# A two-layer diffusion backbone on one core: another list scheduler for every engine but TensorE

## The chip, the cores and the metric

The kernel runs on one core of one Trainium2 chip. The metric is the device time of one execution in microseconds (us); lower is better. Each time is the median of several runs, and one more execution is recorded by the hardware profiler.

## The reference

Two layers work on 512 latent tokens `x` and 256 context tokens `ctx`, with a width of 1024. Each layer modulates its input by rows made from a conditioning vector, mixes tokens by attention, normalises, and then does the same around an MLP:

```python
for i in range(2):
    mod_x = silu(c) @ w_ada[i] + b_ada[i]            # 6 rows of 1024: shift, scale, gate, twice
    mod_c = silu(c_ctx) @ w_ada[i] + b_ada[i]
    hx, hc = x * (1 + sc1) + sh1, ctx * (1 + csc1) + csh1
    if i == 0: ax, ac = window_gqa(hx, hc, ...)      # 16 heads on 2 KV heads, band of 128, a sink logit
    else:      ax, ac = diff_attention(hx, hc, ...)  # 8 heads, softmax minus lambda times softmax
    x  = layer_norm(alpha * x + g1 * ax)
    fx = square(relu((x * (1 + sc2) + sh2) @ w1[i])) @ w2[i]
    x  = layer_norm(alpha * x + g2 * fx)
    # the context tokens take the same path in layer 0; layer 1 needs only x
```

## The kernel before

**Products.** Matmuls are float32 with both operands split into a rounded part and a rest. `wsplit` (line 302) loads a weight piece `w_raw` by DMA, makes the rounded part `w_h` by a copy on ScalarE (recorded at the helper's line 264), and the rest `w_l = w_raw - w_h` on VectorE (line 314). `mm3` (lines 325 to 327) issues the three matmuls of such a product. Loads use three buffers (`NRAW`), so a load is issued when an earlier piece has been split. In the first MLP the pieces are combined first: `w_half` and `w_sum` are such combinations, and `hx0m`, `hx_sum` and `hid` the activations' parts.

**Stages.** In the order of the profile: loads and modulation rows of layer 0 (to about 75 us), layer-0 attention (to 341), layer norm (to 381), first MLP (to 870) with the modulation rows of layer 1 done beside it, layer norm and the first projection of layer 1 (to 905), layer-1 attention (to 1285), layer norm (to 1330), second MLP (to the end).

**Layer norm.** The tokens are six tiles of 128 (`acc0_3734` to `acc0_3739` are the tiles of the layer-0 residual at the first norm, `acc0_7901` to `acc0_7906` at the second, `acc1_12804` to `acc1_12807` the four of layer 1). A sublayer's result in PSUM is multiplied by the gate (`g_tmp`, line 583, VectorE) and added to `acc`, on VectorE or POOL; BN_STATS, BN_AGGR and `rstd` give the moments (the power is on POOL); line 534 normalises the tile on VectorE; line 549 transposes it on TensorE (`xn_t`); ScalarE modulates the transposed tile (`fx`, `hx_v`) and rounds it (`hx0m`, `hx1`, `hx1m`), and VectorE makes the rest under the same name. `acc0 * g10 + g11` (line 672) makes the scaled residual afterwards.

**Modulation rows.** For layer 1 they are computed on VectorE beside the first MLP: each of 56 loads of `w_adaT` into `w_raw` is multiplied by the broadcast conditioning rows `cB0` and `cB1` and summed along the row (`ada_pr` or `w_raw`, an instruction printed as ISA in the order and as CUSTOM_DVE in the profile, then a read of its accumulator into `mods1` or `ada_half`).

**Attention of layer 1.** `sk` and `sq` are the rotated keys and queries, made on VectorE from `rope1`; line 1654 transposes `sk` on TensorE (`kT_ps`).

**What sets the order.** Each engine works through one row of instructions in program order. The row of TensorE is written out by the kernel's own planner (`Flow`), and is kept as written:

```python
ctx.enter_context(tc.manual_schedule(engines={mybir.EngineType.PE}))
```

The rows of VectorE (DVE), ScalarE (ACT), POOL and SyncE (SP, which issues the DMAs) are chosen by the framework's scheduler, which goes through all instructions with estimated times and picks, engine by engine, which of those that are ready goes next. A few hints (`add_manual_dep`) fix the order of single pairs.

## Time and profile before

| | us |
|---|---|
| median of 3 runs | 1657.44 (1653.25 to 1660.99) |
| profiled execution, its time | 1661.91 |
| its span in the profile | 1660.1 |
| TensorE (PE) busy | 1582.9 |
| VectorE (DVE) busy | 1134.4 |
| ScalarE (ACT) busy | 794.1 |
| POOL busy | 447.4 |
| moved by DMA | 181.17 MB |

The span is the time from the first to the last instruction of the profile; the rest of the execution's time lies around it. TensorE is busy for most of the span, so a time is lost where TensorE waits. In the lists of waits a row names the waiting engine with its line, what it waited for, the sum of the waits in us, how often, and the longest. In a timeline a row has its start, its length, engine, line, operation, and in brackets the idle time ahead of it with the instruction that ended it.

### The profile page before, as it was taken

What the parts mean: (1) busy time and instruction counts of PE and PEld (TensorE: products, weight loads), DVE (VectorE), ACT (ScalarE), POOL (GpSimd) and SP (SyncE); (2) the same over time, 40 slices, a digit from 0 to 9 for tenths busy, and PEclk for the clock granted to TensorE, in tenths of its full rate; (3) what the DMA queues carried; (4) which work ended last, traced back from release to release, by engine and by line L of the source; (5) the groups of instructions that cost most, each with busy time, mean ns of one, the idle gap of its engine ahead of it and who ended that gap; (6) DMA issues with size and microseconds to landing.
All of it is one profiled execution on the core that took longest, in us unless ns stands there. A gap on an engine that the chain in (4) does not pass through costs nothing.

```text
span 1660.1 us, 25174 instructions
## 1 busy us (share of the span) xinstructions
PE 1582.9 (95%) x9465; PEld 1384.8 (83%) x9465; DVE 1134.4 (68%) x2201; ACT 794.1 (48%) x1683; POOL 447.4 (27%) x369
## 2 busy tenths in 40 slices
PE   7899999989999999999997999999989799999998
PEld 5788777789788888889986999899877788888896
DVE  4655676689776688766566777677664886666667
ACT  3455675365343344334416555555552745555550
POOL 1333554106111121211191222220100033333363
PEclk9999999999999999999998999999899999999999
DMA  9110550533354434443323122211123233333221
GB/s 373 41 52 33 179 178 26 197 127 128 131 173 150 142 105 161 153 140 114 126 69 114 49 72 66 73 47 39 48 69 135 89 115 115 102 102 100 99 70 63
DMA packets 66434, 181.17 MB, mean 109 GB/s; under 512 B 7368, under 2 KB 13320, under 8 KB 66312
## 3 DMA queue, kind: packets, MB, share of 16 engines
q1 hardware_dynamic: 66312, 179.56, 32.0%
q8 instruction: 74, 1.21, 0.3%
q14 instruction: 48, 0.39, 0.1%
HBM read 168.49 MB, written 11.04 MB: 108 GB/s over the span
## 4 chain that ended last, share of the span: by engine, by line
PE 64%; DVE 14%; issue 7%; DMA 6%; POOL 5%; ACT 4%; SPq 0%; DVEq 0%; POOLq 0%; ACTq 0%
PE y_ps L327 8%; PE y_ps L325 8%; PE y_ps L326 7%; PE h_ps L325 6%; PE h_ps L326 6%; PE h_ps L327 6%; DMA w_raw<-in_w_adaT 3%; PE qkv_ps L325 2%; PE qkv_ps L326 2%; PE qkv_ps L327 2%; PE o_ps L1371 2%; PE s_ps L1750 2%; PE pT_ps L1389 2%; DVE w_l L314 2%; DVE w_raw L260 2%
## 5 line engine op out<-in xcount | busy, mean ns | idle before, releaser
L325 PE MATMUL y_ps<-w_h,hid 128*128 128x512 f32 (+1 forms) x648 | 257.4, 397 | 3.2 <-DVE fx L260 2.1
L327 PE MATMUL y_ps<-w_h,hid 128*128 128x512 f32 (+1 forms) x648 | 256.6, 396 | 2.7 <-DVE hid L260 2.6
L326 PE MATMUL y_ps<-w_l,hid 128*128 128x512 f32 (+1 forms) x648 | 255.8, 395 | 0.0
L314 DVE TENSOR_TENSOR w_l<-w_raw,w_h 128x1024 fp32r<-128x1024 f32 (+1 forms) x133 | 159.2, 1208 | 52.5 <-ACT w_h L264 49.9
L264 ACT CAST w_h<-w_raw 128x1024 fp32r<-128x1024 f32 (+1 forms) x133 | 131.2, 1001 | 94.8 <-PE y_ps L327 64.7
L264 ACT CAST w_half<-w_raw 128x512 fp32r<-128x512 f32 x130 | 80.3, 621 | 151.6 <-PE h_ps L327 106.2
L327 PEld LDWEIGHTS y_ps<-w_h,hid 128*128 128x128 f32 x648 | 122.8, 189 | 33.4 <-DVE hid L260 4.5
L325 PEld LDWEIGHTS y_ps<-w_h,hid 128*128 128x128 f32 x648 | 123.1, 190 | 29.1 <-DVE fx L260 2.5
L326 PEld LDWEIGHTS y_ps<-w_l,hid 128*128 128x128 f32 x648 | 123.1, 190 | 24.7
L260 DVE TENSOR_TENSOR w_half<-w_raw,w_half 128x512 fp32r<-128x512 f32 x130 | 106.6, 825 | 54.2 <-ACT w_half L264 53.8
L268 POOL TENSOR_TENSOR w_sum<-w_raw 128x512 f32<-128x512 f32 x26 | 58.2, 2238 | 316.9 <-DMA w_raw<-in_w 203.4
L325 PE MATMUL qkv_ps<-w_h,hx 128*128 128x384 f32 (+1 forms) x384 | 128.8, 335 | 2.8 <-ACT w_h L264 2.7
L326 PE MATMUL qkv_ps<-w_l,hx 128*128 128x384 f32 (+1 forms) x384 | 124.0, 323 | 2.0 <-DVE w_l L314 2.0
L327 PE MATMUL qkv_ps<-w_h,hx 128*128 128x384 f32 (+1 forms) x384 | 123.7, 322 | 0.0
L268 POOL TENSOR_TENSOR e<-e,sm 128x512 f32<-128x512 f32 (+2 forms) x96 | 92.6, 976 | 109.2 <-DVE sm L260 84.1
L260 DVE CUSTOM_DVE_ANT_0 w_raw<-w_raw,cB 128x512 f32<-128x512 f32 x112 | 83.1, 769 | 47.4 <-DMA w_raw<-in_w_adaT 47.2
L264 ACT ACTIVATE relu<-relu 128x384 f32<-128x384 f32 (+3 forms) x104 | 69.8, 673 | 64.5 <-DVE relu L260 62.9
L260 DVE TENSOR_TENSOR fx<-y_ps,fx 128x512 f32<-128x512 f32 x110 | 75.0, 686 | 36.9 <-PE y_ps L327 36.8
L268 POOL TENSOR_TENSOR rope<-rope,rope 128x256 f32<-128x256 f32 (+1 forms) x40 | 33.8, 846 | 224.7 <-DVE rope L260 178.0
L268 POOL TENSOR_TENSOR w_raw<-w_raw,w_sum 128x512 f32<-128x512 f32 x26 | 37.6, 1445 | 177.0 <-DVE w_half L260 154.7
L264 ACT ACTIVATE e<-e,nm 128x513 f32<-128x513 f32 (+2 forms) x96 | 65.9, 688 | 33.0 <-DVE nm L260 26.3
L325 PEld LDWEIGHTS qkv_ps<-w_h,hx 128*128 128x128 f32 x384 | 73.4, 191 | 4.6 <-ACT w_h L264 2.9
(268 smaller groups left out, 4323.5 us busy)
## 6 DMA issues: line engine op xcount, KB each, us to landing
w_raw<-in_w SPq DMA_DIRECT2D x128, 512.0 KB, 3.6
w_raw<-in_w_adaT SPq DMA_DIRECT2D x56, 512.0 KB, 3.8
w_raw<-in_w_ada SPq DMA_DIRECT2D x24, 512.0 KB, 4.3
w_raw<-in_b_w SPq DMA_DIRECT2D x32, 384.0 KB, 3.4
raw<-in_w_ada SPq DMA_DIRECT2D x16, 512.0 KB, 9.3
w_raw<-in_a_wq SPq DMA_DIRECT2D x8, 512.0 KB, 8.1
w_raw<-in_a_wo SPq DMA_DIRECT2D x8, 512.0 KB, 4.5
w_raw<-in_b_wo SPq DMA_DIRECT2D x8, 512.0 KB, 4.1
```

What stands on the lines that cost most here:

```text
L260: fn(**kw)
L264: fn(**kw)
L268: fn(**kw)
L314: last["split"] = nc.vector.tensor_tensor(**kw)
L325: nc.tensor.matmul(out=o, lhsT=lh, rhs=rh, start=start, stop=False, **kw)
L326: nc.tensor.matmul(out=o, lhsT=lh, rhs=rl, start=False, stop=False, **kw)
L327: last["pe"] = nc.tensor.matmul(out=o, lhsT=ll, rhs=rh, start=False, stop=stop, **kw)
L1371: nc.tensor.matmul(out=po[odd * HD:odd * HD + HD, 0:256], lhsT=vv[:, kb, kvh], rhs=pt_[:, odd * 256:odd * 256 + 256], start=(i == 0), stop ...
L1389: nc.tensor.transpose(out=pp[:, c * P:(c + 1) * P], in_=es[j][:, i * P:(i + 1) * P], identity=ident)
L1750: nc.tensor.matmul(out=sp[:, c * 512:c * 512 + 384], lhsT=qTt[:, tt, hl, qb * P:(qb + 1) * P], rhs=kS[:, tt, c * 384:c * 384 + 384], start ...
```

## The change

The scheduler is told to keep its time with its finer timeline model instead of its coarse one:

```diff
-    with tile.TileContext(nc) as tc:
+    with tile.TileContext(nc, schedule_with_timeline_sim=True) as tc:
```

The instructions stay the same, and so does TensorE's row. On the other engines the rows are permuted: nearly all of the difference is the place at which an instruction stands. Three places follow.

**VectorE at the norm before the first MLP.** `acc0_3739` is the last of the six tiles. Before, its statistics and its normalisation (last row) stood thus:

```order
L260 BN_STATS bn_3694<-acc0_3739 128x6
L260 TENSOR_TENSOR hx0m_3761<-fx_3765,hx0m_3761 128x2x128 x4
L260 BN_AGGR mv_4086<-bn_3694 128x2
L260 TENSOR_TENSOR fx_3762<-fx_3765,fx_3762 128x512
L260 TENSOR_SCALAR g11_3742<-g11_3742 128x1024
L260 TENSOR_SCALAR rstd_4088<-mv_4086 128x1
L260 TENSOR_TENSOR hx0m_3761<-fx_3766,hx0m_3761 128x2x128
L534 TENSOR_SCALAR acc0_3739<-acc0_3739,mv_4086,rstd_4088 128x1024
```

Now, from the row in which a weight split has come in:

```order
L314 TENSOR_TENSOR w_l_4410<-w_raw_4408,w_h_4409 128x1024
L260 TENSOR_TENSOR hx0m_3761<-fx_3765,hx0m_3761 128x2x128
L260 BN_AGGR mv_4086<-bn_3694 128x2
L260 TENSOR_TENSOR hx0m_3761<-fx_3765,hx0m_3761 128x2x128
L260 TENSOR_TENSOR fx_3765<-fx_3765 128x512
L260 TENSOR_SCALAR g11_3742<-g11_3742 128x1024
L260 TENSOR_TENSOR fx_3763<-fx_3766,fx_3763 128x512
L672 TENSOR_TENSOR acc0_3734<-acc0_3734,g10_3740 128x1024
L260 TENSOR_SCALAR rstd_4088<-mv_4086 128x1
L260 TENSOR_TENSOR fx_3765<-fx_3765,fx_3762 128x512
L260 TENSOR_TENSOR hx0m_3761<-fx_3766,hx0m_3761 128x2x128 x4
L260 TENSOR_TENSOR acc0_3734<-acc0_3734,g11_3742 128x1024
```

The normalisation of `acc0_3739` is the row behind the last one shown; ahead of it have come `w_l_4410`, the scaled residual of another tile (`acc0_3734`), steps of `fx`, and three more of `hx0m`.

**VectorE in the first MLP.** `relu_4778` and `relu_4777` are parts of the hidden activations, `w_raw_5164` is one of the 56 modulation loads. Before:

```order
L260 TENSOR_TENSOR relu_4778<-h_ps_4863,relu_4778 128x384
L260 TENSOR_TENSOR w_half_4939<-w_sum_4336,w_half_4939 128x512
L260 ISA w_raw_5142,mods1_82<-w_raw_5142,cB1_4675 128x512
L260 ISA mods1_82 128x1
L314 TENSOR_TENSOR w_l_4944<-w_raw_4942,w_h_4943 128x1024
L260 ISA ada_pr_5166,mods1_82<-w_raw_5164,cB0_4674 128x512
```

Now:

```order
L260 ISA ada_pr_5166,mods1_82<-w_raw_5164,cB0_4674 128x512
L260 ISA mods1_82 128x1
L260 ISA ada_pr_5168,mods1_82<-w_raw_5164,cB0_4674 128x512
L260 ISA mods1_82 128x1
L260 ISA w_raw_5164,mods1_82<-w_raw_5164,cB1_4675 128x512
L260 ISA mods1_82 128x1
L260 ISA w_raw_5164,mods1_82<-w_raw_5164,cB1_4675 128x512
L260 ISA mods1_82 128x1
L260 TENSOR_TENSOR relu_4778<-h_ps_4863,relu_4778 128x384
```

All four reductions of `w_raw_5164` have moved from behind `relu_4778` to ahead of it.

**VectorE at the end of layer 0.** `y_ps` are the last results of the first MLP in PSUM, `g20_7999` the gate. Before:

```order
L534 TENSOR_SCALAR acc0_7901<-acc0_7901,mv_8182,rstd_8184 128x1024
L583 TENSOR_TENSOR g_tmp_8200<-y_ps_7986,g20_7999 128x512
L260 BN_STATS bn_8061<-acc0_7902 128x6
L260 BN_AGGR mv_8204<-bn_8061 128x2
L260 TENSOR_SCALAR rstd_8206<-mv_8204 128x1
L583 TENSOR_TENSOR g_tmp_8222<-y_ps_8147,g20_7999 128x512
```

Now:

```order
L583 TENSOR_TENSOR g_tmp_8200<-y_ps_7986,g20_7999 128x512
L260 BN_STATS bn_8133<-acc0_7906 128x6
L583 TENSOR_TENSOR g_tmp_8222<-y_ps_8147,g20_7999 128x512
L260 BN_STATS bn_8043<-acc0_7901 128x6
L260 BN_AGGR mv_8182<-bn_8043 128x2
L260 TENSOR_SCALAR rstd_8184<-mv_8182 128x1
L260 BN_STATS bn_8061<-acc0_7902 128x6
L260 BN_AGGR mv_8204<-bn_8061 128x2
L260 TENSOR_SCALAR rstd_8206<-mv_8204 128x1
L260 BN_STATS bn_8079<-acc0_7903 128x6
L534 TENSOR_SCALAR acc0_7901<-acc0_7901,mv_8182,rstd_8184 128x1024
```

The two products `g_tmp` have moved ahead of the statistics, and the normalisation of `acc0_7901` stands behind the statistics of two further tiles. On ScalarE the casts `w_h_8450`, `w_h_8456`, `w_h_8462` and `w_h_8468` of the next projection's weights moved forward: from behind the fourth tile's steps (the last one from among the fifth's) to between those of the second, third and fourth.

## The prediction

> **What bounds the kernel now.** I read the page's list of busy times first, then the table of stretches, then the waits of TensorE, and last the timelines of the few places where TensorE waits.
>
> ```profile
> PE 1582.9 (95%) x9465; PEld 1384.8 (83%) x9465; DVE 1134.4 (68%) x2201; ACT 794.1 (48%) x1683; POOL 447.4 (27%) x369
> ...
> 0.00:75.00 75.00, 61.98 (x422) 46.27 (x423) 37.01 (x88) 29.52 (x56) 14.94 (x19) 1.00 0.60 229
> 75.00:341.00 266.00, 260.11 (x1805) 203.34 (x1805) 172.03 (x471) 156.52 (x434) 101.94 (x106) 1.00 0.31 106
> 341.00:381.00 40.00, 35.45 (x243) 33.91 (x242) 37.31 (x56) 24.73 (x56) 3.49 (x3) 0.96 0.40 145
> 381.00:870.00 489.00, 478.93 (x2343) 423.95 (x2342) 347.06 (x645) 181.13 (x286) 131.61 (x77) 1.00 0.40 133
> 870.00:905.00 35.00, 24.43 (x107) 19.64 (x106) 24.31 (x51) 22.84 (x63) 8.78 (x10) 0.81 0.24 90
> 905.00:1285.00 380.00, 363.82 (x2363) 338.56 (x2362) 257.29 (x536) 196.15 (x456) 64.04 (x77) 0.98 0.21 69
> 1285.00:1330.00 45.00, 36.06 (x246) 32.93 (x245) 40.31 (x71) 31.49 (x70) 4.46 (x6) 0.91 0.26 86
> 1330.00:1660.10 330.10, 322.10 (x1947) 286.24 (x1946) 219.07 (x288) 151.69 (x266) 118.12 (x75) 0.99 0.29 96
> ```
>
> TensorE is the bound: busy for 1582.9 of 1660.1 us, so all its waits together are 77 us, and a new order elsewhere can gain no more than that. In the table (columns: stretch, its length, busy time of PE, PEld, DVE, ACT, POOL, then clock, DMA share, GB/s) the waits sit in short stretches: 4.6 us around 341 to 381, 10.6 us in 870 to 905, 8.9 us in 1285 to 1330. There VectorE is nearly full (37.31 of 40, 40.31 of 45), so what stands ahead of a waited-for instruction on VectorE counts in full. What TensorE waits for:
>
> ```profile
> PE kT_ps L1654 <- DVE sk L260: 7.8, 6, 2.3
> ...
> PE xn_t L549 <- DVE g_tmp L583: 4.3, 2, 2.8
> PE h_ps L325 <- DVE relu L260: 4.0, 2, 2.7
> PE xn_t L549 <- ACT hx0m L264: 3.6, 1, 3.6
> PE s_ps L1334 <- DVE nm L260: 2.8, 4, 1.1
> PE qkv_ps L325 <- ACT w_h L264: 2.7, 1, 2.7
> PE y_ps L327 <- DVE hid L260: 2.6, 3, 1.1
> PE y_ps L325 <- DVE fx L260: 2.1, 1, 2.1
> PE q_ps L325 <- DVE rope L260: 1.5, 1, 1.5
> ```
>
> **The change part by part.** Every instruction stays; TensorE's row order stays. VectorE, ScalarE, POOL and SP rows are permuted. So no busy time changes, and each edit costs only what it puts ahead of something TensorE waits for, or takes away there. I go through the stretches in order.
>
> *Start and layer-0 attention (0 to 341).* SP now issues the constants (rope tables, mask, sink, the context weights) ahead of two of the input rows, and VectorE has one weight split ahead of the first modulation steps. The added bytes ahead are about 0.7 MB; at the 373 GB/s of the first slice below that is 2 us, and the split of 0.8 to 1.2 us may count too: up to +3, or +5 if a constant that lands late stalls VectorE.
>
> ```profile
> GB/s 373 41 52 33 179 178 26 197 127 128 131 173 150 142 105 161 153 140 114 126 69 114 49 72 66 73 47 39 48 69 135 89 115 115 102 102 100 99 70 63
> ```
>
> Against that the rope multiplication (wait 1.5 us) and three of the four row maxima nm (2.8 us in all) stand 1.5 to 3 us earlier: up to -4. I take -1, range -4 to +5.
>
> *Layer norm before the first MLP (341 to 381).*
>
> ```profile
> 349.03 1.22 DVE L314 TENSOR_TENSOR w_l<-w_raw,w_h 128x1024 fp32r<-128x1024 f32 x1
> ...
> 355.16 0.81 DVE L534 TENSOR_SCALAR acc<-acc,mv,rstd 128x1024 f32<-128x1024 f32 x1 [0.44 <-POOL rstd L268]
> 355.89 0.42 DVE L260 TENSOR_TENSOR hx0m<-fx,hx0m 128x256 fp32r<-128x256 f32 x1
> 356.23 1.22 DVE L672 TENSOR_TENSOR acc<-acc,g 128x1024 f32<-128x1024 f32 x1
> ...
> 356.08 1.30 PE L549 MATMUL xn_t<-identr,acc 128*128 128x128 f32 x5 [3.60 <-ACT hx0m L264]
> ```
>
> TensorE stands 3.60 us until 356.08; the view names hx0m, but the normalisation of acc0_3739 ends 0.1 us earlier and is the real last one. The new order puts ahead of it: w_l_4410 (1.22), the products acc0_3734 by g10 and plus g11 (1.22 each), fx_3763 and two steps of fx_3765 (0.7 each), and three more hx0m sums (0.34 from one start to the next); fx_3762 is ahead in both. Sum 3.7 + 2.1 + 1.0 = 6.8. Of this 1 to 1.5 us goes into idle slots that VectorE has now (0.44 before the normalisation, 0.77 for g11). It ends near 361.5: **+5.5**. The first matmuls that use this tile come 11 us later, with slack, so nothing covers or doubles it. Low end +3, if the added steps fill all of VectorE's waits there; high end +8, if g11 comes late behind the two broadcast loads (cB) now issued ahead of it.
>
> *First MLP (381 to 870).* Beside it VectorE reduces modulation rows (ada_pr and w_raw, with the small reads of the accumulator) from 56 loads:
>
> ```profile
> w_raw<-in_w_adaT SPq DMA_DIRECT2D x56, 512.0 KB, 3.8
> ...
> DVE w_raw L260 <- DMA w_raw<-in_w_adaT: 47.2, 26, 3.6
> DVE ada_pr L260 <- DMA w_raw<-in_w_adaT: 21.8, 10, 4.7
> ...
> 452.63 0.55 DVE L260 TENSOR_TENSOR relu<-h_ps,relu 128x384 f32<-128x384 f32 x1
> 458.23 0.69 DVE L260 CUSTOM_DVE_ANT_0 ada_pr<-w_raw,cB 128x512 f32<-128x512 f32 x1 [1.81 <-DMA w_raw<-in_w_adaT]
> 458.85 0.08 DVE L260 DVE_READ_ACCUMULATOR2_ANT mods<- 128x1 f32 x1
> ...
> 453.24 0.44 PE L325 MATMUL h_ps<-hx0m,w_half 128*128 128x384 f32 x1 [2.74 <-DVE relu L260]
> ```
>
> A load is issued when the last reduction of an earlier one frees its buffer, and lands 3.8 us later; VectorE already stands 69.0 us (47.2 + 21.8) for these landings. The new order pulls reductions ahead of MLP steps. At 453 the four of w_raw_5164 (0.77 each with the read, 3.1 us) now stand ahead of relu_4778, behind a load that has no other VectorE work to cover its 3.8 us; done with the landing of before (458.2) the relu would end 8.7 us later than now. Adding up, over all 56 loads, what is left of 3.8 us after the VectorE work between release and first use gives about 12 us more standing than before. But VectorE is idle for 142 us of this stretch, and a TensorE that is 5.5 us late already gives it that lead: the +6 us that the same count gives at 425 (w_half_4642) falls into this lead. What stays are the places with no slack: 453 (+3), the hid sums at 464 to 468 (+1), 597 (+1) and 660 (+2), the fx at 711 (+1). **+8**; low end 0 (the lead is enough everywhere), high end +20 (the 12 us of standing plus the 8 us of work all reach TensorE).
>
> *End of layer 0 (870 to 905).*
>
> ```profile
> 885.72 1.11 PE L549 MATMUL xn_t<-identr,acc 128*128 128x128 f32 x4 [2.76 <-DVE g_tmp L583]
> ...
> 887.49 0.63 PE L327 MATMUL y_ps<-w_h,hid 128*128 128x512 f32 x1
> ...
> 891.97 0.39 PE L327 MATMUL y_ps<-w_h,hid 128*128 128x512 f32 x1
> ...
> 897.41 2.41 ACT L264 CAST w_h<-w_raw 128x768 fp32r<-128x768 f32 x3
> ...
> 898.41 0.58 PE L325 MATMUL qkv_ps<-w_h,hx 128*128 128x384 f32 x1 [2.71 <-ACT w_h L264]
> ```
>
> Here the order helps. The gated products g_tmp, whose PSUM results are ready long before, move ahead of the layer-norm steps, so POOL's adds and with them the later norms start earlier: up to 4.3 us of waits on g_tmp. The casts w_h for the next projection, which now hold qkv_ps for 2.71 us, move 20 rows and more forward on ScalarE. In exchange the same casts (0.8 us each) stand between the transposed tiles' steps, the first norm waits for a third tile's statistics, and one cast, w_h_8468, now waits for a load in front of tiles. Gains 4.3 + 2.7, losses about 3: **-4**; ends -8 (no loss, and 1 us of the slow matmuls recovered) and +2 (ScalarE stands 3 us for that load, twice).
>
> The rows at 887.49 and 891.97 show the same kind of matmul at 0.63 and 0.39 us: for about 5 us after the wait of 2.76 TensorE ran slow (clock 0.81 over the stretch). After the 2.74 us at 453 it did not. So a new wait may bring slow matmuls with it; rival (d) prices that.
>
> *Layer-1 attention (905 to 1285).* The six waits on sk (7.8 us) are the tight places.
>
> ```profile
> 928.82 0.96 DVE L314 TENSOR_TENSOR w_l<-w_raw,w_h 128x768 fp32r<-128x768 f32 x1
> ```
>
> At five of them the new order puts one such split (0.96) ahead of sk: +4.8. At one, near 1040, sk moves ahead of a 1.0 us step: -1.5 with what moved before it. Three pT copies swap with a row maximum: +0.4 each. **+4**, range 0 to +8.
>
> *Layer norm before the second MLP (1285 to 1330).*
>
> ```profile
> 1295.05 0.81 DVE L534 TENSOR_SCALAR acc<-acc,mv,rstd 128x1024 f32<-128x1024 f32 x1 [0.35 <-POOL rstd L268]
> ...
> 1296.38 1.22 DVE L314 TENSOR_TENSOR w_l<-w_raw,w_h 128x1024 fp32r<-128x1024 f32 x1
> ...
> 1301.91 0.58 PE L326 MATMUL h_ps<-hx1m,w_h 128*128 128x256 f32 x1 [1.93 <-DVE hx1m L260]
> ```
>
> Four splits (1.22 each) that followed it move ahead of the normalisation at 1295.05: +4.9, so it ends near 1300.3 and its transposes come 5 us late. The last of the four needs a load that goes out only when the first has run; that one moves forward as well, so the load comes in time. But TensorE waited here for the hx1m sums of the earlier tiles, until 1301.91. Those move by 2.4 to 3 us, and the splits are not needed again afterwards. **+3**, range 0 to +8 (all of the delay, and 3 us of ScalarE standing for the load).
>
> *Second MLP (1330 to the end).* The orders nearly agree and there are no modulation rows: 0.
>
> Sum: -1 + 5.5 + 8 - 4 + 4 + 3 = +15.5. The profiled execution took 1661.9 us (span 1660.1), so its changed twin would take 1677.4. It was 4.5 us above the median of the runs, 1657.4; against the median the same sum is **1673 us**.
>
> **The rivals.** (a) *The lead absorbs it.* Each delay of TensorE gives VectorE, idle for a third of the span, time to run ahead. If the first norm's 5.5 us covers the whole MLP and layer 1's splits fall into idle slots, what is left is -1 + 5.5 - 4 + 0 to 5: about 1657 to 1663, no measurable change. For it: 142 us of idle VectorE in the MLP. Against: 69.0 us of these are standing at loads, which a lead shortens only where the buffer is free earlier.
>
> (b) *Faster: the end of layer 0 decides.* In 870 to 905 TensorE stands 10.6 us and runs slow. If the earlier g_tmp and w_h clear all of that, it gains 10.6 us and 2.4 us of slow matmuls (12 at 0.2), -13. With the first norm at its low end, +3, and the start at its, -4, and nothing in the MLP, the time is 1643. The point is where the other delays stay under 5 us. Against it: the norms in that stretch also wait for POOL's adds, whose work stays.
>
> (c) *Much slower: loads stop VectorE in the MLP.* If the standing of 12 us and the work ahead reach TensorE in full, +20 there instead of +8, with the rest at its upper half (+13): 1690.
>
> (d) *The new waits slow TensorE.* As at 887, a new wait would be followed by some 12 matmuls that start 0.2 us further apart, 2.4 us. The first norm's wait has this now, but three new waits (453, 660, 1296) would make +7: 1680. Against: at 453 a wait as long was not followed by it. The Trainium skill, "TensorE: Matmul & The Clock Gate", Part 1: The HAM clock gate, says that the clock is halved after an idle window of about 3.4 us and comes back after as long a busy one. By that rule only those new waits that grow past 3.4 us pay, about 1.7 us each (an estimate from the page), so the sum would be 2 to 5 us higher. The trace disagrees on the threshold: a wait of 2.76 us was followed by slow matmuls.
>
> That nothing happens because the order is the same is excluded by the lists of rows.
>
> **How the numbers follow.** Chances: my forecast with its neighbours, 1666 to 1685, 0.42; (d) 0.08; (c) 0.16; (a) 0.24; (b) 0.10. The single forecast is 1673; the range from 1649 to 1695 leaves out (b) below its bound and the top of (c). What a measurement of this kernel can tell from no change is about 0.5%, or 8.3 us: faster means below 1649, slower above 1666. So faster 0.10, same 0.24, slower 0.66.
>
> **What would show it.** In the changed profile: the transposes at the first norm wait 8 to 10 us instead of 3.60; the wait on relu in the first MLP grows from 2.7 to 5 us or more and waits on hid and fx add up to over 8 us; VectorE's standing at the in_w_adaT loads grows from 69 to about 80 us; the waits on g_tmp and on w_h in 870 to 905 shrink below 3 us; the six on sk grow to 11 us or so. I am wrong if VectorE's steps stay covered in 381 to 870 (then (a)), or if a stall at a load that I did not see holds ScalarE or VectorE for 5 us or more.

## The result and the profile after

The changed kernel takes 1674.53 us (1670.37 to 1678.85, four runs) against 1657.18 us for the kernel before on the same chip: a ratio of 1.0092, 95% interval 1.0068 to 1.0115. It is slower by 17 us, as forecast in sign and nearly in size (1673). Its profiled execution took 1678.85 us with a span of 1677.1.

The first row is from the page's list of busy times; the others are the table of stretches, cut so that each stretch holds the same TensorE work as the stretches shown of before (columns as there).

```profile
PE 1587.7 (95%) x9465; PEld 1390.5 (83%) x9465; DVE 1143.6 (68%) x2201; ACT 795.5 (47%) x1683; POOL 443.7 (26%) x369
...
0.00:72.10 72.10, 61.48 (x422) 46.17 (x423) 35.88 (x87) 29.72 (x57) 15.00 (x18) 1.00 0.63 238
72.10:334.90 262.80, 259.50 (x1806) 203.16 (x1806) 175.94 (x473) 155.93 (x433) 105.28 (x106) 1.00 0.32 107
334.90:382.30 47.40, 37.99 (x243) 36.47 (x242) 44.31 (x65) 26.00 (x59) 2.60 (x3) 0.86 0.41 145
382.30:884.00 501.70, 485.02 (x2343) 428.51 (x2342) 344.27 (x647) 181.33 (x284) 124.89 (x82) 0.98 0.39 128
884.00:911.40 27.40, 21.13 (x107) 17.22 (x106) 19.38 (x38) 22.26 (x62) 5.24 (x6) 0.87 0.47 160
911.40:1302.00 390.60, 365.04 (x2363) 340.31 (x2362) 258.17 (x537) 198.29 (x457) 65.26 (x77) 0.97 0.20 64
1302.00:1347.60 45.60, 36.14 (x246) 33.44 (x245) 39.47 (x70) 30.73 (x68) 5.35 (x4) 0.89 0.25 81
1347.60:1677.10 329.50, 321.44 (x1947) 285.22 (x1945) 226.21 (x289) 151.28 (x267) 120.09 (x75) 0.99 0.30 96
```

Take the second column of a row here and of its twin there. The start and layer-0 attention (the first two rows together) are 6.1 us shorter, the first norm 7.4 longer, the first MLP 12.7 longer, the end of layer 0 7.6 shorter, layer-1 attention 10.6 longer, the rest the same: together 17.0 in this pair of executions. No engine's busy time moved by more than 1% (VectorE 1134.4 to 1143.6). But TensorE's rose by 4.9 us for the same matmuls, and in the first MLP by 6.1 (478.93 to 485.02) at a clock of 0.98 instead of 1.00: there only 6.6 of the 12.7 us are waits. What TensorE waits for, and then two rows of VectorE's own waits:

```profile
PE kT_ps L1654 <- DVE sk L260: 13.1, 8, 2.6
PE xn_t L549 <- issue: 7.5, 1, 7.5
PE xn_t L549 <- ACT fx L264: 6.2, 2, 4.3
PE y_ps L327 <- DVE hid L260: 6.0, 3, 4.0
...
PE y_ps L325 <- ACT hid L264: 4.4, 1, 4.4
PE xn_t L549 <- DVE acc L534: 4.3, 2, 2.4
PE h_ps L325 <- DVE relu L260: 3.9, 3, 3.2
PE y_ps L325 <- DVE g_tmp L583: 3.9, 3, 2.0
PE xn_t L549 <- ACT hx_v L264: 3.7, 1, 3.7
...
PE s_ps L1334 <- DVE nm L260: 0.4, 1, 0.4
```

```profile
DVE w_raw L260 <- DMA w_raw<-in_w_adaT: 48.8, 28, 3.5
...
DVE ada_pr L260 <- DMA w_raw<-in_w_adaT: 33.1, 17, 4.5
```

The wait on the rope product at the start has gone (1.5 us before), and of that on `nm` 0.4 us is left (2.8 before). The wait for the last tile at the first norm has grown from 3.6 to 7.5 us. New are two long waits on `hid` and one of 4.3 us on `fx` at the last norm; those on `sk` have grown. VectorE stands 81.9 us at the modulation loads, where it stood 69.0.

### The profile page after: what moved, and what is told of

It is laid out like the page before. It is cut to its first block, busy times and chain, and to the rows that moved or that the text cites. A ratio compares the mean times of both kernels' runs of the same rounds, so it can differ in the third digit from the quotient of the medians.

```text
span 1677.1 us, 25186 instructions
## 1 busy us (share of the span) xinstructions
PE 1587.7 (95%) x9465; PEld 1390.5 (83%) x9465; DVE 1143.6 (68%) x2201; ACT 795.5 (47%) x1683; POOL 443.7 (26%) x369
## 3 DMA queue, kind: packets, MB, share of 16 engines
q8 instruction: 74, 1.21, 0.3%
## 5 line engine op out<-in xcount | busy, mean ns | idle before, releaser
L260 DVE TENSOR_TENSOR w_half<-w_raw,w_half 128x512 fp32r<-128x512 f32 x130 | 111.4, 859 | 46.0 <-ACT w_half L264 44.8
L268 POOL TENSOR_TENSOR w_sum<-w_raw 128x512 f32<-128x512 f32 x26 | 49.3, 1898 | 338.2 <-DMA w_raw<-in_w 225.2
L260 DVE CUSTOM_DVE_ANT_0 w_raw<-w_raw,cB 128x512 f32<-128x512 f32 x112 | 78.8, 732 | 48.8 <-DMA w_raw<-in_w_adaT 48.8
L264 ACT COPY relu<-h_ps 128x384 f32<-128x384 f32 (+1 forms) x78 | 33.1, 424 | 99.6 <-PE h_ps L327 85.0
```

The source lines that it names most:

```text
L260: fn(**kw)
L264: fn(**kw)
L268: fn(**kw)
```

## The experiments

**How the kernels were made.** A function after the kernel's body ties the instructions of each row to one another, so that the scheduler has no choice; the rows (one list each for VectorE, ScalarE, POOL and SP) are taken stretch by stretch from the order of before or from that of the change. Nothing else is edited. A kernel with every row tied in the old order was not run; but in the eight kernels with the old rest, that stretch differs from the kernel before by -0.5 to +0.8 us, so the ties show no cost of their own there.

```diff
+def put_in_order(tc, nc):
+    ins = {i.name: i for i in nc.cur_bb.bb.instructions}
+    for row in ROWS:
+        row = [f"I-{n}" for n in row if f"I-{n}" in ins]
+        for a, b in zip(row, row[1:]):
+            tc.add_manual_dep(ins[b], a, ORDER, reason="row order")
...
     with tile.TileContext(nc) as tc:
         hybrid_block(tc, t, out)
+        put_in_order(tc, nc)
```

The stretches by the time in the profile before: start (0 to 341, with layer-0 attention), norm (to 398), MLP (to 851), end of layer 0 (to 905), attention (to 1286), rest. An edit is written below as the order that each stretch takes. All times are medians, each with the kernel before on the same chip. Where a stretch is named "longer" or "shorter", the start of one matmul in two profiled executions is compared. Single executions differ here: between 905 and 1285 seven kernels with the old order were 4.6 us shorter to 0.8 us longer than the profiled execution of before. Less than about 4 us in one pair decides nothing in that stretch; there the medians do.

**1. Start alone.**

```diff
-start old | norm old | MLP old | end old | attention old | rest old
+start new | norm old | MLP old | end old | attention old | rest old
```

> The new order only up to the end of the layer-0 attention (341 us), the old one behind it. Theory A, places add up: each place costs or gives what it shows in the changed profile, whatever stands elsewhere. TensorE was 6.1 us ahead at 341 there, so 6 us faster, about 1651. Theory B, the lead: a gain for TensorE is a loss of lead for VectorE, which is nearly full in the norm behind; the 6 us shrink to 0 to 3 us, about 1655.

Measured: 1653.07 against 1658.72, ratio 0.9971 (0.9958 to 0.9983): 5.7 us faster. The loss of up to 3 us that the prediction allowed for the constants issued ahead of the input rows did not come; the gains on the rope product and the row maxima did.

**2. End of layer 0 alone.**

```diff
-start old | norm old | MLP old | end old | attention old | rest old
+start old | norm old | MLP old | end new | attention old | rest old
```

> The new order only from 851 to 905 us (end of layer 0, first projection of layer 1), the old one elsewhere. Theory A: in the changed profile TensorE made up 6 us between these two points, so 6 us faster, about 1651. Theory B: it made them up because it came 12 us late and POOL's adds, which wait for little of TensorE's, were done; with TensorE on time they are not, so 0 to 3 us faster, about 1656.

Measured: 1654.92 against 1658.72, ratio 0.9984 (0.9969 to 0.9999): 3.8 us faster, 4.7 in the stretch (851 to 905). Over the same rows the whole change is 6.1 us shorter (7.6 from 870 on).

**3. First MLP alone.**

```diff
-start old | norm old | MLP old | end old | attention old | rest old
+start old | norm old | MLP new | end old | attention old | rest old
```

> The new order only in the first MLP (398 to 851 us), the old one elsewhere. Theory A: the changed profile lost 11 us between these points, so 11 us slower, about 1668. Theory B: there the MLP began with TensorE 7 us late against the norm's start, which gave VectorE a lead; without it the places at 425, 453 and 464 to 468 cost what they cost by their rows, so 15 to 18 us slower, about 1673.

Measured: 1683.12 against 1658.72, ratio 1.0151 (1.0128 to 1.0173): 24 us slower, more than either theory said. The part costs more alone than the whole change. Between 398 and 851, where the rows are new, it is 17.2 us longer (the complete change: 11.2). Another 8.4 us come between 851 and 870, among old rows:

```profile
879.95 1.74 DVE L260 TENSOR_TENSOR acc<-acc,g_tmp 128x512 f32<-128x512 f32 x1 [6.07 <-POOL acc L268]
...
883.95 0.79 PE L326 MATMUL y_ps<-w_l,hid 128*128 128x512 f32 x1 [6.33 <-DVE w_l L314]
```

VectorE stands at an add, for POOL, ahead of the split that TensorE needs. Near there POOL's new row makes eight products `fx` before its first add, where the old one takes two of each by turns, so the adds for which VectorE's old row waits come later. Neither the kernel before nor the complete change has this wait, so it belongs to the seam of the two orders. Then, from 870 to 905, the kernel is 8.7 us shorter. TensorE's waits in that stretch of this kernel (the list of waits, 899.7 to 926.1 us):

```profile
PE qkv_ps L325 <- ACT w_h L264: 2.9, 1, 2.9
PE qkv_ps L326 <- DVE w_l L314: 1.2, 1, 1.2
PE xn_t L549 <- DVE g_tmp L583: 1.1, 1, 1.1
PE xn_t L549 <- ACT hx_v L264: 0.3, 1, 0.3
```

That is 5.5 us where the kernel before waits 10.6. The waits on `g_tmp` (4.3 before) and `rstd` (2.1) are almost gone with no row moved, because the other engines have caught up with a TensorE that comes late. But this only gives back what was lost just ahead: over 851 to 905 together the old rows are 0.3 us shorter. The new end does gain more where TensorE comes late: 6.1 to 8.3 us behind the new MLP rows (the complete change and runs 5, 6, 7 and 12), 4.5 to 4.8 behind the old ones (runs 2, 10 and 11).

**4. First norm alone.**

```diff
-start old | norm old | MLP old | end old | attention old | rest old
+start old | norm new | MLP old | end old | attention old | rest old
```

> The new order only in the norm before the first MLP (341 to 398 us), the old one elsewhere. Theory A: 7.4 us slower as in the changed profile, about 1665. Theory B: the 7 us give VectorE a lead in the MLP behind, where TensorE waits 9.8 us in all in the old order; most of these waits go, so only 0 to 4 us slower, about 1659.

Measured: 1662.98 against 1658.72, ratio 1.0029 (1.0010 to 1.0047): 4.3 us slower; TensorE's wait for the last tile's transposes is 8.7 us and the norm 6.7 longer. The term stands (5.5). Whether a part of the 6.7 is taken back later isn't shown: the one large gain behind it in the pair, 4.4 us, is in attention, inside the spread named above.

**5. Everything but the norm.**

```diff
-start new | norm new | MLP new | end new | attention new | rest new
+start new | norm old | MLP new | end new | attention new | rest new
```

> The new order everywhere but in the norm before the first MLP (341 to 398 us), which has the old one. Theory A, places add up: the 7.4 us lost there come back, 1667. Theory B, the lead: without them TensorE comes to the first MLP on time, the wait at 425 us (w_half) of about 6 us appears that the full change does not show, and at most 2 us are gained: 1673 to 1676.

Measured: 1681.13 against 1660.51, ratio 1.0122 (1.0101 to 1.0143). Taking away a part that costs 4.3 us alone brings nothing: the kernel is, if anything, slower than the complete change (1.0092; the intervals overlap a little). Its profile shows the wait that the prediction had kept out of its sum, on `w_half` near 425. The matmul in the timeline:

```profile
431.13 0.69 PE L327 MATMUL h_ps<-hx0m,w_half 128*128 128x384 f32 x1 [8.55 <-DVE w_half L260]
```

Two things can explain that the complete change lacks it: with the new norm TensorE comes later there, or the splits pulled forward at the norm free the load buffers and the modulation loads run earlier. Both are in the profiles. VectorE's first reduction here, and then in the complete change:

```profile
400.83 0.69 DVE L260 CUSTOM_DVE_ANT_0 ada_pr<-w_raw,cB 128x512 f32<-128x512 f32 x1 [4.21 <-DMA w_raw<-in_w_adaT]
```

```profile
396.56 0.69 DVE L260 CUSTOM_DVE_ANT_0 ada_pr<-w_raw,cB 128x512 f32<-128x512 f32 x1
```

It comes 4.3 us earlier with the new norm, and without a wait. Run 6 takes the two apart.

**6. The whole change, but the normalisation first at the norm.** The early splits stay early; only the last tile's statistics and normalisation move ahead of them.

```diff
 L260 SCALAR_TENSOR_TENSOR acc0_3739<-acc0_3739,g_tmp_4046 128x512
+L260 BN_STATS bn_3694<-acc0_3739 128x6
+L260 BN_AGGR mv_4086<-bn_3694 128x2
+L260 TENSOR_SCALAR rstd_4088<-mv_4086 128x1
+L260 TENSOR_TENSOR hx0m_3761<-fx_3765,hx0m_3761 128x2x128 x2
+L534 TENSOR_SCALAR acc0_3739<-acc0_3739,mv_4086,rstd_4088 128x1024
 L260 TENSOR_TENSOR fx_3762<-fx_3765,fx_3762 128x512
...
 L260 TENSOR_TENSOR acc0_3734<-acc0_3734,g11_3742 128x1024
-L534 TENSOR_SCALAR acc0_3739<-acc0_3739,mv_4086,rstd_4088 128x1024
```

> The complete new order, but at the first norm of layer 0 VectorE takes bn_3694, mv_4086, rstd_4088 and the normalisation of acc0_3739 directly behind acc0_3739's last add, ahead of the splits (w_l_4410 and its neighbours) that the new order had put there. The other engines and everything behind are as in the changed kernel. Theory 'chain of loads': those splits free the raw buffers, and with them the first modulation loads of the MLP, so early that w_half at 425 does not wait; the splits are only some 5 us later now, still far ahead of the old order. So the norm gains about 5 us and nothing comes back at 425: the ratio to the kernel before falls from 1.0092 to about 1.006 (1667 to 1670 us). Theory 'TensorE's lag' (the prediction's: the wait at 425 is not seen because TensorE itself comes late from the norm): whatever the norm gains, w_half at 425 waits as much longer, 5 us or more, and the time stays at 1673 to 1677.

Measured: 1676.52 against 1659.48, ratio 1.0089 (1.0067 to 1.0112): no gain. In the profile it is there and goes again. First the complete change: VectorE's rows at the norm, the transposes that wait for them, and the later load and `w_half`.

```profile
349.96 0.69 DVE L260 TENSOR_SCALAR g<-g 128x1024 f32<-128x1024 f32 x1 [1.65 <-DMA g<-in_lnrow]
...
355.45 0.80 DVE L534 TENSOR_SCALAR acc<-acc,mv,rstd 128x1024 f32<-128x1024 f32 x1
...
356.36 1.94 PE L549 MATMUL xn_t<-identr,acc 128*128 128x128 f32 x8 [7.47 <-issue]
...
422.46 0.69 DVE L260 CUSTOM_DVE_ANT_0 ada_pr<-w_raw,cB 128x512 f32<-128x512 f32 x1 [1.11 <-DMA w_raw<-in_w_adaT]
...
425.64 0.68 DVE L260 TENSOR_TENSOR w_half<-w_raw,w_half 128x512 fp32r<-128x512 f32 x1
```

And with the normalisation first:

```profile
347.37 0.81 DVE L534 TENSOR_SCALAR acc<-acc,mv,rstd 128x1024 f32<-128x1024 f32 x1
...
350.24 1.04 PE L549 MATMUL xn_t<-identr,acc 128*128 128x128 f32 x8
...
421.03 0.69 DVE L260 CUSTOM_DVE_ANT_0 ada_pr<-w_raw,cB 128x512 f32<-128x512 f32 x1 [1.28 <-DMA w_raw<-in_w_adaT]
...
424.21 0.69 DVE L260 TENSOR_TENSOR w_half<-w_raw,w_half 128x512 fp32r<-128x512 f32 x1
...
424.95 0.69 PE L327 MATMUL h_ps<-hx0m,w_half 128*128 128x384 f32 x1 [5.67 <-DVE w_half L260]
```

The transposes no longer wait: TensorE gains 7.6 us at the norm. At `w_half` it loses 5.7 of it, since the load on which VectorE stands comes only 1.4 us earlier (421.03 against 422.46), and at the end of the kernel 0.8 us are left of the gain. So the norm's delay is free here because the chain of loads, and of the VectorE steps that free their buffers, sets the time behind it. This is the lead of the prediction. The earlier loads count as well, though they don't let TensorE through by themselves: for that matmul VectorE's `w_half` ends at 431.1 in run 5 and at 426.3 in the complete change, 4.8 us earlier, and TensorE comes there 3.8 us later (422.6 and 426.4). Together that is about the 8.55 us.

**7. Everything but the place at 660.** The rows of VectorE, ScalarE and SP from 644 to 686 us in the old order, the two modulation loads' reductions again behind the MLP steps.

```diff
-start new | norm new | MLP new                                 | end new | attention new | rest new
+start new | norm new | MLP new to 644, old to 686, new to 851 | end new | attention new | rest new
```

> The new order everywhere but between 644 and 686 us of the first MLP, which has the old one (VectorE, ScalarE, SP). Theory A: the two new waits for hid at 660 (4.4 and 4.0 us) go, 8 to 9 us faster than the full change, 1666. Theory B: a part comes back as waits further on (at 711 and 883 us the changed profile made up time because TensorE was late), so 4 to 6 us faster, 1670.

Measured: 1673.67 against 1660.51, ratio 1.0074 (1.0050 to 1.0098), against 1.0092: by the ratios 3 us less, inside the intervals. The place is plain in the profile of the complete change. VectorE, with one row of ScalarE:

```profile
653.74 0.89 DVE L260 CUSTOM_DVE_ANT_0 ada_pr<-w_raw,cB 128x512 f32<-128x512 f32 x1 [2.07 <-DMA w_raw<-in_w_adaT]
...
660.44 0.84 ACT L264 ACTIVATE relu<-relu 128x768 f32<-128x768 f32 x1 [6.88 <-DVE relu L260]
...
663.87 0.69 DVE L260 CUSTOM_DVE_ANT_0 ada_pr<-w_raw,cB 128x512 f32<-128x512 f32 x1 [2.86 <-DMA w_raw<-in_w_adaT]
...
668.15 0.69 DVE L260 TENSOR_TENSOR w_half<-w_raw,w_half 128x512 fp32r<-128x512 f32 x1
668.76 0.95 DVE L260 TENSOR_TENSOR hid<-relu,hid 128x768 fp32r<-128x768 f32 x1
```

and TensorE:

```profile
664.94 0.51 PE L325 MATMUL y_ps<-w_h,hid 128*128 128x512 f32 x1 [4.36 <-ACT hid L264]
...
669.76 0.79 PE L327 MATMUL y_ps<-w_h,hid 128*128 128x512 f32 x1 [4.00 <-DVE hid L260]
670.36 0.63 PE L325 MATMUL y_ps<-w_h,hid 128*128 128x512 f32 x1
...
675.81 0.39 PE L326 MATMUL y_ps<-w_l,hid 128*128 128x512 f32 x1
```

Before the first of these waits, VectorE stands 2.07 us at one load and does its reductions and two splits ahead of the `relu` for which ScalarE then stands 6.88 us. Before the second it stands 2.86 us at the next load and does the reductions and two `w_half` ahead of the `hid` that TensorE needs. That makes 8.4 us of waits, and 12 matmuls at 0.63 us behind them. With the old rows the waits there fall to 3.0 us (0.80, 0.29, 1.21, 0.72).

**8. Attention alone.**

```diff
-start old | norm old | MLP old | end old | attention old | rest old
+start old | norm old | MLP old | end old | attention new | rest old
```

> The new order only in the layer-1 attention (905 to 1286 us), the old one elsewhere. Theory A: the changed profile lost 10.6 us there, so 1668. Theory B: here TensorE and VectorE wait for each other at every block, so there is no lead to absorb a split ahead of sk, and the loss does not shrink when the stretch stands alone: also 10 or more, up to 14. The count of rows in the prediction gave 4 us: 1662.

Measured: 1668.81 against 1660.51, ratio 1.0053 (1.0035 to 1.0071): 8.3 us slower, twice the prediction's term.

**9. Attention alone, the splits behind `sk`.** All six places like this one:

```diff
 L260 TENSOR_TENSOR vt1_11933<-qkv_ps_12368,vt1_11933 128x128
+L260 TENSOR_TENSOR sk_12399<-qkv_ps_12368,sk_12399 128x2x64
 L314 TENSOR_TENSOR w_l_12422<-w_raw_12420,w_h_12421 128x1024
-L260 TENSOR_TENSOR sk_12399<-qkv_ps_12368,sk_12399 128x2x64
```

> The new order in layer-1 attention alone (905 to 1286 us), but the six weight splits w_l that the new order has put just ahead of a sk stand behind that sk again. Theory 'a split in front of sk' (the prediction's reason for attention): of the 8.3 us that the new order costs there, 5 to 7 go (the rises at 928, 1053, 1057, 1222, 1227): ratio about 1.001, 1661 us. Rival 'later in general' (VectorE's other moves, row maxima and pT copies, cost as much): the ratio stays above 1.003, 1664 or more.

Measured: 1668.05 against 1659.48, ratio 1.0050 (1.0031 to 1.0069). The theory falls: nothing that can be measured comes back. The profile of this kernel shows why. ScalarE, then VectorE and TensorE, at the sixth place:

```profile
1227.36 1.04 ACT L264 CAST w_h<-w_raw 128x1024 fp32r<-128x1024 f32 x1 [2.21 <-DMA w_raw<-in_b_wo]
1228.31 0.26 ACT L264 CAST sk<-qkv_ps 128x128 fp32r<-128x128 f32 x1
...
1228.60 0.29 DVE L260 TENSOR_TENSOR sk<-qkv_ps,sk 128x128 fp32r<-128x128 f32 x1 [2.15 <-ACT sk L264]
...
1229.04 0.34 PE L1654 MATMUL kT_ps<-identr,sk 128*128 128x128 f32 x2 [3.03 <-DVE sk L260]
```

In the kernel before:

```profile
1226.07 0.27 ACT L264 CAST sk<-qkv_ps 128x128 fp32r<-128x128 f32 x1 [0.38 <-DVE vt L260]
...
1228.15 1.05 ACT L264 CAST w_h<-w_raw 128x1024 fp32r<-128x1024 f32 x1
...
1227.51 0.34 PE L1654 MATMUL kT_ps<-identr,sk 128*128 128x128 f32 x2 [1.41 <-DVE sk L260]
```

VectorE's `sk` follows ScalarE's half of `sk`, and the new order has put a weight cast ahead of that too, which stands 2.21 us at a load. With the split out of VectorE's way `sk` waits for ScalarE instead, and TensorE waits 3.03 us where it waited 1.41. Over the stretch the waits on `sk` are 7.8 us in the kernel before, 12.9 in run 8 and 11.1 here. And 5.5 us of waits that the kernel before lacks are not on `sk` and are the same in runs 8 and 9: 3.0 on `pT` in four places, 1.6 on `g_tmp` and 0.9 on `rope`. That is the rival written down ahead of the run, VectorE's other moves. A cast ahead of ScalarE's `sk` was not moved back in a run of its own, nor were these moves, so how the 8.3 us divide stays open.

**10. Start and end of layer 0.**

```diff
-start old | norm old | MLP old | end old | attention old | rest old
+start new | norm old | MLP old | end new | attention old | rest old
```

> The new order up to 341 us and from 851 to 905 us, the old one elsewhere: the two stretches that gained when tried alone. Theory A: their gains add, 5 + 3 us, about 1650. Theory B: the first gain takes lead away from VectorE and POOL before the second, so 5 to 6 us in all, about 1653.

Measured: 1650.27 against 1660.51, ratio 0.9935 (0.9915 to 0.9955). The two gains add (5.7 + 3.8 = 9.5; measured 10.2). It beats both kernels.

**11. The same with the new norm, normalisation first.**

```diff
-start new | norm old                      | MLP old | end new | attention old | rest old
+start new | norm new, normalisation first | MLP old | end new | attention old | rest old
```

> The new order at the start and in layer-0 attention, at the first norm (with the normalisation first, as in the run above) and at the end of layer 0; the old order in both MLPs, in layer-1 attention and at the last norm. Theory 'chain of loads': the early splits at the norm pay also with the old order behind them, so this is 2 to 5 us below the kernel with the start and the end of layer 0 alone (ratio 0.9935): 1644 to 1648, ratio 0.991 to 0.993. Theory 'places add': the norm with the normalisation first costs nothing and brings nothing, ratio 0.9935, 1650. If the norm still costs its 5 us, 1655.

Measured: 1649.69 against 1659.48, ratio 0.9939 (0.9922 to 0.9956), the same as run 10. With the old MLP rows, earlier loads bring nothing that the medians show.

**12. The whole change with three places mended.**

```diff
-start new | norm new                      | MLP new                                | end new | attention new | rest new
+start new | norm new, normalisation first | MLP new to 644, old to 686, new to 851 | end new | attention old | rest new
```

> The complete new order but for three places: the normalisation first at the first norm of layer 0, the old order from 644 to 686 us of the first MLP (the modulation reductions at 660), and the old order in layer-1 attention. If the three costs are the ones found and go without coming back elsewhere, 5 + 4 + 9 us come off the changed kernel's 1674.5: 1656 or 1657, ratio 0.998 to 1.000. If, as with the places tried alone, a part of each comes back at the next wait, 1660 to 1665, ratio 1.002 to 1.004.

Measured: 1663.72 against 1659.48, ratio 1.0026 (1.0010 to 1.0041). The second case holds: 11 of 18 us. The gain at the norm comes back on `w_half` again (its longest wait there is 6.8 us), that of attention stays: against the complete change the stretch is 12.1 us shorter.

## Why the prediction was right, and where its terms were not

The time and the mechanism were right: the same instructions in another order cost what they put ahead of something that TensorE waits for. The one part of the mechanism that was put at nothing is TensorE's busy time, which rose by 4.9 of the 17.0 us. But the sum came out partly because errors cancelled. Term by term, forecast and then measured in the pair of profiled executions, and alone by medians where it was run:

| term | forecast | in the pair | alone |
|---|---|---|---|
| start and layer-0 attention | -1 (-4 to +5) | -6.1 | -5.7 |
| first norm | +5.5 (+3 to +8) | +7.4 | +4.3 |
| first MLP | +8 (0 to +20) | +12.7 | +24.4 |
| end of layer 0 | -4 (-8 to +2) | -7.6 | -3.8 |
| layer-1 attention | +4 (0 to +8) | +10.6 | +8.3 |
| last norm and rest | +3 (0 to +8) | 0.0 | |
| sum | +15.5 | +17.0 | +27.5 |

*The start* was mis-sized by 5 us, below its own range: the price for constants ahead of input rows (+3) was a bound from bytes, and no wait answers to it.

*The first norm* was nearly right. Its wait is 7.47 us, just below the 8 to 10 expected, so 3.9 more than before. Of the 7.4 us in the pair 2.5 are not waits: TensorE is busy that much longer (35.45 to 37.99 us, at a clock of 0.86 instead of 0.96), which the term had not. One step was priced low: `g11`, ahead of the normalisation in both orders, now stands 1.65 us for its load (0.77 before), the high end of the term's own reasoning.

*The first MLP.* The step that failed is the list of places. At 453 the forecast was +3 and the wait grew from 2.74 to 3.15; the `hid` sums at 464 to 468 came 3.0 us better, not 1 worse; 597 was +2.4 for +1; the `fx` at 711 was 1.6 better, not 1 worse; and 660 was +8.8, not +2. The wait on `g_tmp` at 862.69 (2.04) was not on the list. And the sum priced waits alone, where nearly half of the stretch's loss is slow matmuls (rival (d) below): at 453 the wait grew by 0.4 us, but the matmuls behind it lost 2.7. The count of standing at loads was good (81.9 us, about 80 forecast), but which of it reaches TensorE was not to be had from a count. The step that the delay near 425 falls into the lead was right, as run 6 shows, and it was the step that mattered: without the norm's delay 5.7 to 8.5 us come up there. But the earlier loads do as much as TensorE's coming late (4.8 and 3.8 us), and the prediction had only the second.

*The end of layer 0.* The waits on `g_tmp` and `w_h` are gone from the list there, as forecast; two others, 3.7 on `hx_v` and 2.4 on the normalisation, stand in their place. The forecast of -4 is what the order is worth (3.8 alone). Of the further 3.8 us in the table, 1.5 only give back what was lost between 851 and 870; the rest goes with a TensorE that comes late, as the groups under run 3 show. In single executions this is small.

*Attention.* Twice the forecast, at or beyond the end of its range. The sign and the place (`sk`, 13.1 us for 11) were right; the reason, VectorE's splits, was not enough: run 9. The `pT` copies were priced at 0.4 each, 1.2 in all, and the waits on them are 3.0. The order of ScalarE was not priced there at all.

*The last norm* was priced at +3 and cost next to nothing: two matmuls near 1294 and 1296 come 2.0 and 3.1 us later, and 3.4 of it is back by 1302.

*The rivals.* (a) was half right: between 398 and 851 the new MLP rows cost 11.2 us behind the delayed norm, and 16.6 to 19.3 where the norm is not delayed (runs 3, 5 and 6). The lead takes a part, not all. (b) needed the start's gain and no loss in the MLP; the gains were there (runs 1, 2 and 10), the condition wasn't. (c), 20 us in the MLP, is nearer to the MLP alone (24.4) than to the complete change. (d) came in part: counting the `h_ps` and `y_ps` matmuls whose starts lie further apart than usual, TensorE lost 7.0 us in four places (near 455, 670, 863 and 1242), against 2.3 in two before (468 and 887). One of them stands in the rows of run 7. Another, in the complete change:

```profile
862.69 0.50 PE L325 MATMUL y_ps<-w_h,hid 128*128 128x512 f32 x1 [2.04 <-DVE g_tmp L583]
...
863.98 0.63 PE L326 MATMUL y_ps<-w_l,hid 128*128 128x512 f32 x1
...
866.91 0.40 PE L327 MATMUL y_ps<-w_h,hid 128*128 128x512 f32 x1
```

A wait of 2.04 us was followed by about 3 us of slow matmuls (granted clock 0.50 from 863.4 to 866.8), while after the 2.74 us at 453 in the kernel before there were none. The Trainium skill, "TensorE: Matmul & The Clock Gate", Part 1: The HAM clock gate, ties the slow clock to an idle window of about 3.4 us; the length of the slow part agrees roughly, the length of the wait does not. The sum had none of the 4.7 us of difference.

## What to carry to other kernels

Price a reordering by place, and then ask at each place what sets the time behind it: a delay in front of a chain of loads is free up to the lead of that chain, and a gain there is given back (7.6 us won, 0.8 left). Parts of an order don't add: +27.5 us as parts, +17 as a whole, also because a part tried alone can wait at its seams (8.4 us in run 3), so undo a part in the complete change as well as doing it alone. Where an awaited result is made by two engines, look at what stands ahead on both; taking it away on one alone showed nothing.

## What the runs showed that was not expected

A part of an order tried alone brought a wait that neither whole order has, 6.33 us at its seam in run 3; most of what the stretch behind it then gained was this delay given back. A scheduler's order can be split by stretches: keeping the new one only where it gains (runs 10 and 11) gives 1650 us, ratio 0.9935, where the complete one gives 1.0092. And one stretch of 380 us varied by 5 us between executions of kernels with the same rows in it, so a term of that size needs medians, not one pair of traces.
